# Down projection of a decoder layer: a third piece in four by seven products, some subtractions on GpSimd

## The chip, the cores and the metric

One core of one Trainium2 chip runs one decoder layer on 256 positions. The metric is the device time of one execution in microseconds, median of three runs. TensorE does the matmuls, VectorE (DVE) and ScalarE (ACT) the elementwise work, GpSimd (POOL) a little, and SyncE (SP) issues nearly all DMAs.

## What is computed

```
x <- LayerNorm(ALPHA * x + token_mixer(x))          # three branches, then w_out
x <- LayerNorm(ALPHA * x + swiglu_ffn(x))

def swiglu_ffn(x, w_gu, w_down):
    gate, up = split(x @ w_gu, 2)                   # 2048 -> 2 x 5632
    return (silu(gate) * up) @ w_down               # 5632 -> 2048
```

All is float32, and only the last line, the down projection of the feed-forward part, changes in how it is computed.

## The kernel before

**Matmuls in split form.** Each float32 operand is split into a high part (rounded to the fp32r format, by a ScalarE copy) and a low part (operand minus high part, a VectorE subtraction). A product is three matmuls: high by high, high by low, low by high.

**Pieces.** All weights stream through as pieces of 256 rows by 512 columns, laid out as 128 x 1024 (512 KB). A `Job` is a run of pieces with one accumulator. One list, `pieces`, fixes the order of the whole program; nothing is reordered later. For piece i the main loop does, in this order: issue loads (`advance`), split the piece three ahead (`advance_split`; its high part is copied one piece earlier still), the matmuls of piece i (`mults`), one waiting small task (`later`), and, at the last piece of a job, its evacuation (`job.evac`). VectorE and ScalarE work through their instructions in this order. There are 6 buffers for raw pieces, 5 for high parts (`wh`) and 4 for low parts (`wl`), so the low part of a piece can be written when the piece four before it has been multiplied.

**The feed-forward stage.** The hidden width is cut into 11 blocks of 512. Block b has a gate job and an up job of 8 pieces each (form A). From block 2 on, `weave` (L1062) puts four pieces of the down projection (form B) into each such job, one after every second piece: blocks 2 and 3 carry the down pieces of the hidden pair 0 and 1, blocks 4 and 5 those of the pair 2 and 3, and so on, one quarter of the 2048 output columns per job. That makes 18 woven jobs. The rest of the down projection follows by itself at the end (`down`, L1051).

**Seven products.** An ordinary form-B piece multiplies a 256 x 256 block of the hidden values by a 256 x 512 block of weights with 12 matmuls of 512 columns (`mul_b`, L1159). Two of the four down pieces of a woven job, k = 1 and 2, instead use Strassen's seven products of 128 x 128 by 128 x 256 (`mul_seven`, L1185), 21 matmuls of 256 columns. This needs sums of the four weight blocks, which `split_lo` (L1129) makes on VectorE (L1145 to L1147), splits (L1148, and `split_from` twice, L203 and L204) and puts into a slot that alternates between `h0` and `s5`; and sums of the hidden blocks, which `ev_ffup` makes for odd blocks only (`sums`, L895 to L903). Even blocks only split their hidden values.

**Accumulators.** PSUM has three double banks `acc` and two single banks `tr`. A woven job's form-A part uses two of the `acc`. Its down part uses the third (`ab`) and, for the seven products, both `tr` banks (`c` and `d`, taken by the first product piece). `ev_seven` (L928) evacuates them: L935 (L933 for the first pair) adds `ab`; L937 copies `d` on ScalarE; L939 to L941 form differences; L942 adds the first half of `c`, which is the last read of that bank; L943 and L944 add the rest. The first matmul of `mul_seven` writes `c`.

**At the end of a job** the order of VectorE's work is: evacuation of the form-A part (L616, for an up job with L889), split of the next job's first down piece, for an up job the split or the sums of the first half of its hidden values, and then `ev_seven`.

Of the kernel before, what the change touches and what calls it, by code (L numbers as in the profile page):

```python
# [12 lines left out]
F32R = mybir.dt.float32r  # L13
I32 = mybir.dt.int32
AF = mybir.ActivationFunctionType
ALU = mybir.AluOpType
# [3 lines left out]
P = 128  # L20
NT = 2
T = 256
KT = D // P
DFF = 5632
NB = DFF // 512
# [23 lines left out]
class Job:  # L49
    def __init__(self, form, src, act, n, evac, needs=None, bias=None, done=None, post=None, late=None, own=None, banks=False, split=False, seven=()):  # L50
        self.form = form
        self.src = src
        self.act = act
        self.n = n
        self.evac = evac
        self.needs = needs or {}
        self.post = post or {}
        self.bias = bias
        self.done = done
        self.ps = [None, None]  # L60
        self.cd = None
        self.bc = None
        self.late = late or ()
        self.own = own or {}
        self.banks = banks
        self.split = split
        self.seven = seven


class Act:  # L70
# [35 lines left out]
def layer_kernel(ctx: ExitStack, tc: tile.TileContext, xT_d, mem_d, memT_d, wi_d, wif_d, wkv_d,  # L106
                 wpa_d, wpb_d, wpc_d, wout_d, wgu_d, wdn_d, pp_d, bif_d, gws_d, gbs_d, bin_d, gln_d, xr_d, lnp_d, out_d):
    nc = tc.nc
    ve, ac, te, gp, sy = nc.vector, nc.scalar, nc.tensor, nc.gpsimd, nc.sync
# [12 lines left out]
    def nm(s):  # L122
        cnt[0] += 1
        return f"{s}{cnt[0]}"

    def slot(tag, shape, dt=F32):
        return big.tile(shape, dt, tag=tag, name=nm(tag))

    def t2(shape=None, dt=F32):
        return tmp.tile(shape or [P, 512], dt, tag="t2", name=nm("t2"))  # L130
# [4 lines left out]
    def bc2():  # L135
        return tmp.tile([P, 512], F32, tag="bc", name=nm("bc"), bufs=2)
# [7 lines left out]
    def two(a):  # L144
        return a.rearrange("p (a b) -> p a b", a=2)

    def flat(a):
        return a.rearrange("p a b -> p (a b)")
# [53 lines left out]
    def split_from(src, hi_ap, lo_ap):  # L202
        ac.activation(hi_ap, src, AF.Copy)  # L203
        ve.tensor_sub(lo_ap, src, hi_ap)  # L204
# [49 lines left out]
    S = {}  # L254
# [370 lines left out]
    def once(key, make):  # L625
        if key not in S:
            S[key] = make()
        return S[key]
# [243 lines left out]

    later = []

    def ev_ffup(b):
        def f(job, hf):
            g = S["hid", b][:, 2 * hf:2 * hf + 2]
            odd = b % 2
            if hf == 0:
                if odd:  # L880
                    h = slot(("s3", "s1")[b // 2 % 2], [P, 2, 2, 8, P], F32R)
                else:
                    h = slot(("s6", "s6b")[b // 2 % 2], [P, 2, 2, 2, T], F32R)
                for i in range(2):
                    S["hT", b, i] = h[:, i]
            h = S["hT", b, hf]
            u = two(t2())
            comb(job, hf, u)
            ve.tensor_mul(g, g, u)  # L889
            if h.shape[2] != 8:  # L890
                later.append(lambda: split_from(g, h[:, :, 0], h[:, :, 1]))
                return
            a = flat(g).rearrange("p (a b) -> p a b", a=4)

            def sums():  # L895
                ac.activation(h[:, 0, 0:4], a, AF.Copy)
                s = t2([P, 4, P])
                ve.tensor_tensor(s[:, 0:2], a[:, 1:2].to_broadcast([P, 2, P]), a[:, 0:4:3], ALU.subtract)
                ve.tensor_sub(s[:, 2], a[:, 0], s[:, 1])
                ve.tensor_sub(s[:, 3], a[:, 2], s[:, 2])  # L900
                ac.activation(h[:, 0, 4:8], s, AF.Copy)
                ve.tensor_sub(h[:, 1, 0:4], a, h[:, 0, 0:4])
                later.insert(0, lambda: ve.tensor_sub(h[:, 1, 4:8], s, h[:, 0, 4:8]))  # L903

            later.append(sums)
        return halves(f)

    def ev_down(b, j, first, last):
# [19 lines left out]
    def ev_seven(j, first):  # L928
        def f(job):
            a = S["acc"][:, :, j * 512:(j + 1) * 512]  # L930
            ab, (c, d) = job.ps[0], job.cd
            if first:
                ve.scalar_tensor_tensor(a, a, ALPHA, ab, ALU.mult, ALU.add)  # L933
            else:
                ve.tensor_add(a, a, ab)  # L935
            e = t2()
            ac.activation(e, d, AF.Copy)  # L937
            w, z = t2(), t2([P, 2, T])
            ve.tensor_sub(w[:, 0:T], c[:, 0:T], e[:, 0:T])  # L939
            ve.tensor_sub(w[:, T:], w[:, 0:T], e[:, T:])  # L940
            ve.tensor_tensor(z, c[:, T:].unsqueeze(1).to_broadcast([P, 2, T]), two(w), ALU.subtract)  # L941
            ve.tensor_add(a[:, 0, T:], a[:, 0, T:], c[:, 0:T])  # L942
            ve.tensor_add(a[:, 1, T:], a[:, 1, T:], w[:, T:])  # L943
            ve.tensor_add(a[:, :, 0:T], a[:, :, 0:T], z)  # L944
        return f
# [115 lines left out]

    def weave(up, b0, j):  # L1062

        act = lambda: Hid([S["hT", b0, 0], S["hT", b0 + 1, 0], S["hT", b0 + 1, 1], S["hT", b0, 1]])
        src = [wdn_d[j, 2 * b0 + i] for i in (0, 2, 3, 1)]
        dn = Job("B", src, act, 4, ev_seven(j, b0 == 0), seven=(1, 2))
        for k in range(8):
            pieces.append((up, k))
            if k % 2 == 1:
                pieces.append((dn, k // 2))  # L1070

    for b in range(NB):
        n = {k: (lambda kk: (lambda: x1_unit(kk + 2)))(k) for k in range(6)} if b == 0 else None
        gate = Job("A", wgu_d[b], lazy("x1T"), 8, ev_ffgate(b), post=n, done=start("x1", task_x1) if b == 0 else None)
        up = Job("A", wgu_d[NB + b], lazy("x1T"), 8, ev_ffup(b), needs={7: lambda: drain("x1")} if b == 1 else None)
# [9 lines left out]
    raw, hl, owned, cur, n7 = {}, {}, {}, [0], [0]  # L1085
# [47 lines left out]
    def split_lo(i):  # L1133
        l = owned.pop(i) if i in owned else wp.tile([P, 1024], F32R, tag="wl", name=nm("wl"))
        r = raw.pop(i)
        hl[i][1] = l
        job, k = pieces[i]
        if k not in job.seven:
            ve.tensor_sub(l, r, hl[i][0])  # L1139
            return  # L1140
        n7[0] += 1
        s = slot(("h0", "s5")[n7[0] % 2], [P, 2, 1024], F32R)
        hl[i].append(s)
        p, q = bc2(), bc2()
        ve.tensor_tensor(two(p), r[:, 0:T].unsqueeze(1).to_broadcast([P, 2, T]), two(r[:, T:3 * T]), ALU.add)  # L1145
        ve.tensor_add(q[:, 0:T], p[:, 0:T], r[:, 2 * T:3 * T])
        ve.tensor_add(q[:, T:], q[:, 0:T], r[:, 3 * T:])  # L1147
        ve.tensor_sub(l[:, T:], r[:, T:], hl[i][0][:, T:])  # L1148
        split_from(p, s[:, 0, 0:512], s[:, 1, 0:512])
        split_from(q, s[:, 0, 512:], s[:, 1, 512:])  # L1150
# [6 lines left out]
    def mul_b(job, k, h, l, t, half=None):  # L1157
        a = job.act()
        o, n = 0, 512  # L1159
        if job.split and t == 1:  # L1160
            if half is None:
                mul_b(job, k, h, l, t, 0)
                mul_b(job, k, h, l, t, 1)
                return
            if job.ps[1] is None:
                job.ps[1] = [bank(), bank()]
            ps = job.ps[1][half][:, 0:T]
            o, n = half * T, T
        elif job.banks:
            if job.ps[t] is None:  # L1170
                job.ps[t] = bank()
            ps = job.ps[t]
        else:
            ps = acc(job, 0)[:, t]
        for j in range(2):
            kt = 2 * k + j
            wh, wl = h[:, j * 512 + o:j * 512 + o + n], l[:, j * 512 + o:j * 512 + o + n]
            f, e = k == 0 and j == 0, k == job.n - 1 and j == 1
            te.matmul(ps, a.sta(kt, 0, t), wh, start=f, stop=False)  # L1179
            te.matmul(ps, a.sta(kt, 0, t), wl, start=False, stop=False)  # L1180
            te.matmul(ps, a.sta(kt, 1, t), wh, start=False, stop=e)  # L1181

    def mul_seven(job, k, h, l, s):

        a = job.act().pairs[k]  # L1185
        ab = acc(job, 0)
        first = job.cd is None
        if first:
            job.cd = [bank(), bank()]
        c, d = job.cd  # L1190
        end = k == job.seven[-1]
        w = lambda i: (h[:, i * T:(i + 1) * T], l[:, i * T:(i + 1) * T])
        u = lambda i: (s[:, 0, i * T:(i + 1) * T], s[:, 1, i * T:(i + 1) * T])

        def prod(out, i, b, start=False, stop=False):
            te.matmul(out, a[:, 0, i], b[0], start=start, stop=False)  # L1196
            te.matmul(out, a[:, 0, i], b[1], start=False, stop=False)  # L1197
            te.matmul(out, a[:, 1, i], b[0], start=False, stop=stop)  # L1198

        prod(c[:, 0:T], 0, w(1), start=first)  # L1200
        prod(ab[:, 0, T:], 2, w(3))
        prod(ab[:, 0, 0:T], 7, w(2))
        prod(c[:, T:], 5, u(0), stop=end)
        prod(d[:, T:], 4, u(1), start=first)
        prod(d[:, 0:T], 6, u(2), stop=end)
        prod(ab[:, 1, T:], 3, u(3))

    def mul_a(job, k, h, l, hf, w, j):
        a, kt = job.act(), 2 * k + j
# [80 lines left out]
    for i in range(N):  # L1290
        job, k = pieces[i]
# [79 lines left out]
```

## Time and profile before

| | us |
|---|---|
| median of 3 runs (1840.77 to 1841.02) | 1841.02 |
| the profiled execution | 1840.85 |
| its span, first to last instruction | 1839.1 |
| TensorE busy | 1823.3 (99%) |
| VectorE busy | 1283.1 (70%) |
| ScalarE busy | 945.9 (51%) |
| GpSimd busy | 9.5 (1%) |

The mean granted clock of TensorE is 0.998. A busy share is an average over the run; matmuls are pipelined, so that the durations of neighbouring ones overlap and the interval from start to start is what one costs. VectorE's operations overlap a little too.

### The profile page before, as it was taken

Reading aid. Unit: us, or ns where it says so; the run is one execution under the profiler, and the core shown is the slowest. Engines: PE = TensorE matmul, PEld = TensorE weight load, DVE = VectorE, ACT = ScalarE, POOL = GpSimd, SP = SyncE. Lnnn points to the kernel's source line nnn. Section 1 sums busy time; section 2 is a strip of 40 time slices with the busy share of each in tenths; the row PEclk is TensorE's granted clock in tenths of the full one; section 3 lists DMA queues with packets and bytes.
Section 4 is the critical chain, followed back from the end, with each engine's and each line's share of the span. In section 5 each row is a group of like instructions: output and inputs, shape, how many; then the busy total and the mean of one; then the engine's idle time right before and its main releaser. Section 6 shows DMA issues by size and latency. Waiting matters only on the chain.

```text
span 1839.1 us, 26103 instructions
## 1 busy us (share of the span) xinstructions
PE 1823.3 (99%) x10154; PEld 1575.3 (86%) x10154; DVE 1283.1 (70%) x1741; ACT 945.9 (51%) x1147; POOL 9.5 (1%) x24
## 2 busy tenths in 40 slices
PE   9999999999999999999999999999999999999997
PEld 8888888888888888888888888888888888888886
DVE  6886566557667666565555568577877878878787
ACT  6554465555555555544444355455555555555453
POOL 0000000000000000000000000000000000000001
PEclk9999999999999999999999999999999999999999
DMA  9666555555555555655556645665565565566656
GB/s 373 216 223 189 182 171 165 181 166 189 163 188 162 176 191 164 185 186 169 190 189 239 243 158 172 189 200 184 171 219 171 185 217 181 184 196 197 194 173 182
DMA packets 97627, 352.64 MB, mean 192 GB/s; under 512 B 10848, under 2 KB 11360, under 8 KB 96352
## 3 DMA queue, kind: packets, MB, share of 16 engines
q1 hardware_dynamic: 96496, 348.89, 58.5%
q0 software_dynamic: 576, 1.05, 0.5%
q8 instruction: 79, 1.29, 0.3%
q10 hardware_dynamic: 432, 1.05, 0.2%
q14 instruction: 44, 0.36, 0.1%
HBM read 348.85 MB, written 3.15 MB: 191 GB/s over the span
## 4 chain that ended last, share of the span: by engine, by line
PE 97%; DVE 2%; ACT 0%; DMA 0%; issue 0%; SPq 0%; DVEq 0%; ACTq 0%
PE acc L1214 45%; PE acc L1216 23%; PE acc L1181 7%; PE acc L1180 7%; PE acc L1179 7%; PE tr L1198 1%; PE tr L1196 1%; PE tr L1197 1%; PE acc L1198 1%; PE acc L1197 1%; PE acc L1196 1%; DVE wl L1139 1%; PE tr L198 1%; PE tr L199 0%; PE tr L200 0%; DVE t L841 0%
## 5 line engine op out<-in xcount | busy, mean ns | idle before, releaser
L1214 PE MATMUL acc<-s,wh 128*128 128x512 f32 x3520 | 966.2, 396 | 2.5 <-DVE s L846 1.1
L1139 DVE TENSOR_TENSOR wl<-raw,wh 128x1024 fp32r<-128x1024 f32 x589 | 712.3, 1222 | 362.8 <-PE acc L1216 180.9
L1120 ACT ACTIVATE wh<-raw 128x1024 fp32r<-128x1024 f32 x589 | 618.9, 1058 | 566.0 <-PE acc L1214 344.9
L1214 PEld LDWEIGHTS acc<-s,wh 128*128 128x128 f32 x3520 | 602.5, 188 | 86.6 <-DVE s L846 1.4
L1216 PEld LDWEIGHTS acc<-s,wl 128*128 128x128 f32 x3520 | 542.2, 189 | 80.9 <-DVE wl L1139 0.5
L1216 PE MATMUL acc<-s,wl 128*128 128x256 f32 x3520 | 560.8, 281 | 0.1
L1181 PE MATMUL acc<-wh,s 128*128 128x512 f32 x452 | 179.4, 397 | 0.0
L1179 PE MATMUL acc<-wh,s 128*128 128x512 f32 x452 | 179.0, 396 | 0.0
L1180 PE MATMUL acc<-wl,s 128*128 128x512 f32 x452 | 178.2, 394 | 0.0
L1181 PEld LDWEIGHTS acc<-wh,s 128*128 128x128 f32 x452 | 84.9, 188 | 20.4
L1180 PEld LDWEIGHTS acc<-wl,s 128*128 128x128 f32 x452 | 84.9, 188 | 19.4
L1179 PEld LDWEIGHTS acc<-wh,s 128*128 128x128 f32 x452 | 85.0, 188 | 18.6
L616 DVE TENSOR_TENSOR g<-g,acc 128x512 f32<-128x512 f32 x54 | 37.2, 688 | 50.3 <-ACT g L615 34.6
L615 ACT ACTIVATE g<-acc,pp 128x256 f32<-128x256 f32 x64 | 26.9, 472 | 28.9 <-PE acc L1216 28.9
L1118 ACT ACTIVATE wh<-raw 128x768 fp32r<-128x768 f32 x36 | 30.4, 845 | 18.4 <-PE acc L1214 11.7
L1181 PE MATMUL acc<-wh,s6b 128*128 128x512 f32 x96 | 38.1, 397 | 0.0
L1180 PE MATMUL acc<-wl,s6b 128*128 128x512 f32 x96 | 38.0, 396 | 0.0
L1179 PE MATMUL acc<-wh,s6b 128*128 128x512 f32 x96 | 37.8, 394 | 0.0
L612 ACT ACTIVATE t<-acc 128x512 f32<-128x512 f32 x38 | 22.7, 598 | 27.3 <-PE acc L1216 27.3
L616 DVE TENSOR_TENSOR t<-t,acc 128x512 f32<-128x512 f32 x38 | 26.1, 686 | 13.7 <-ACT t L612 13.7
L1148 DVE TENSOR_TENSOR wl<-raw,wh 128x768 fp32r<-128x768 f32 x36 | 34.3, 953 | 0.8
L203 ACT ACTIVATE s<-bc 128x512 fp32r<-128x512 f32 x36 | 22.8, 633 | 19.3 <-DVE bc L1145 15.2
(336 smaller groups left out, 1505.0 us busy)
## 6 DMA issues: line engine op xcount, KB each, us to landing
raw<-in_wi SPq DMA_DIRECT2D x238, 512.0 KB, 3.7
raw<-in_wgu SPq DMA_DIRECT2D x176, 512.0 KB, 4.2
raw<-in_wdn SPq DMA_DIRECT2D x88, 512.0 KB, 3.8
raw<-in_wkv SPq DMA_DIRECT2D x32, 512.0 KB, 3.6
raw<-in_wpb SPq DMA_DIRECT2D x32, 512.0 KB, 4.4
raw<-in_wout SPq DMA_DIRECT2D x32, 512.0 KB, 3.6
raw<-in_wpa SPq DMA_DIRECT2D x16, 512.0 KB, 3.6
raw<-in_wpc SPq DMA_DIRECT2D x16, 512.0 KB, 3.6
```

The source lines that it names most:

```text
L616: ve.tensor_add(out, out, ps[:, :, 0:T])
L1120: ac.activation(h, r, AF.Copy)
L1139: ve.tensor_sub(l, r, hl[i][0])
L1148: ve.tensor_sub(l[:, T:], r[:, T:], hl[i][0][:, T:])
L1179: te.matmul(ps, a.sta(kt, 0, t), wh, start=f, stop=False)
L1180: te.matmul(ps, a.sta(kt, 0, t), wl, start=False, stop=False)
L1181: te.matmul(ps, a.sta(kt, 1, t), wh, start=False, stop=e)
L1196: te.matmul(out, a[:, 0, i], b[0], start=start, stop=False)
L1197: te.matmul(out, a[:, 0, i], b[1], start=False, stop=False)
L1198: te.matmul(out, a[:, 1, i], b[0], start=False, stop=stop)
L1214: te.matmul(ps, w[:, o:o + P], a.both(kt), start=k == 0 and j == 0, stop=False)
L1216: te.matmul(ps[:, 0:T], w[:, o:o + P], a.hi(kt), start=False, stop=k == job.n - 1 and j == 1)
```

## The change

In woven jobs of the blocks from 4 on (the hidden pairs from block 2 on), the order of the four down pieces becomes (1, 2, 3, 0) and the first three of them go by seven products; the fourth is ordinary. The first product piece starts the accumulator, with start flags on the parts that it writes first, and the ordinary piece splits one of its matmuls into two halves of 256 columns, since one half of that bank has not been written by then. The pair of blocks 0 and 1 keeps its order and its two product pieces. To feed a third product piece, the second half of the hidden values of the blocks 2, 4, 6 and 8 is also kept with its sums; their first half moves into a part of a new tile, `lot`, that takes the whole slot `s5` and also holds every second set of weight sums. In all 18 woven jobs the low parts of the form-A pieces 2 and 3 are subtracted by GpSimd in place of VectorE, and that of the last down piece too where three pieces go by seven products.

```diff
--- before.py
+++ after.py
@@ -65,6 +65,7 @@
         self.banks = banks
         self.split = split
         self.seven = seven
+        self.aside = ()
 
 
 class Act:
@@ -872,17 +873,26 @@
 
     later = []
 
+    def lot():
+        return once("lot", lambda: slot("s5", [P, 4096], F32R))
+
     def ev_ffup(b):
         def f(job, hf):
             g = S["hid", b][:, 2 * hf:2 * hf + 2]
-            odd = b % 2
+            q = b // 2 % 2
             if hf == 0:
-                if odd:
-                    h = slot(("s3", "s1")[b // 2 % 2], [P, 2, 2, 8, P], F32R)
+                if b % 2:
+                    h = slot(("s3", "s1")[q], [P, 2, 2, 8, P], F32R)
+                    hs = h[:, 0], h[:, 1]
+                elif b in (0, NB - 1):
+                    h = slot(("s6", "s6b")[q], [P, 2, 2, 2, T], F32R)
+                    hs = h[:, 0], h[:, 1]
                 else:
-                    h = slot(("s6", "s6b")[b // 2 % 2], [P, 2, 2, 2, T], F32R)
+                    h = slot(("s6", "s6b")[q], [P, 2, 8, P], F32R)
+                    o = (2 + q) * 1024
+                    hs = lot()[:, o:o + 1024].rearrange("p (k a t) -> p k a t", k=2, a=2), h
                 for i in range(2):
-                    S["hT", b, i] = h[:, i]
+                    S["hT", b, i] = hs[i]
             h = S["hT", b, hf]
             u = two(t2())
             comb(job, hf, u)
@@ -1061,9 +1071,12 @@
 
     def weave(up, b0, j):
 
-        act = lambda: Hid([S["hT", b0, 0], S["hT", b0 + 1, 0], S["hT", b0 + 1, 1], S["hT", b0, 1]])
-        src = [wdn_d[j, 2 * b0 + i] for i in (0, 2, 3, 1)]
-        dn = Job("B", src, act, 4, ev_seven(j, b0 == 0), seven=(1, 2))
+        o, seven = ((0, 2, 3, 1), (1, 2)) if b0 == 0 else ((1, 2, 3, 0), (0, 1, 2))
+        act = lambda: Hid([S["hT", b0 + i // 2, i % 2] for i in o])
+        src = [wdn_d[j, 2 * b0 + i] for i in o]
+        dn = Job("B", src, act, 4, ev_seven(j, b0 == 0), seven=seven)
+        up.aside = (2, 3)
+        dn.aside = (3,) if len(seven) == 3 else ()
         for k in range(8):
             pieces.append((up, k))
             if k % 2 == 1:
@@ -1136,10 +1149,13 @@
         hl[i][1] = l
         job, k = pieces[i]
         if k not in job.seven:
-            ve.tensor_sub(l, r, hl[i][0])
+            (gp if k in job.aside else ve).tensor_tensor(l, r, hl[i][0], ALU.subtract)
             return
         n7[0] += 1
-        s = slot(("h0", "s5")[n7[0] % 2], [P, 2, 1024], F32R)
+        if n7[0] % 2:
+            s = lot()[:, 0:2048].rearrange("p (a b) -> p a b", a=2)
+        else:
+            s = slot("h0", [P, 2, 1024], F32R)
         hl[i].append(s)
         p, q = bc2(), bc2()
         ve.tensor_tensor(two(p), r[:, 0:T].unsqueeze(1).to_broadcast([P, 2, T]), two(r[:, T:3 * T]), ALU.add)
@@ -1176,7 +1192,11 @@
             kt = 2 * k + j
             wh, wl = h[:, j * 512 + o:j * 512 + o + n], l[:, j * 512 + o:j * 512 + o + n]
             f, e = k == 0 and j == 0, k == job.n - 1 and j == 1
-            te.matmul(ps, a.sta(kt, 0, t), wh, start=f, stop=False)
+            if 0 in job.seven and t == 1 and j == 0:
+                for x in (0, T):
+                    te.matmul(ps[:, x:x + T], a.sta(kt, 0, t), wh[:, x:x + T], start=False, stop=False)
+            else:
+                te.matmul(ps, a.sta(kt, 0, t), wh, start=f, stop=False)
             te.matmul(ps, a.sta(kt, 0, t), wl, start=False, stop=False)
             te.matmul(ps, a.sta(kt, 1, t), wh, start=False, stop=e)
 
@@ -1184,7 +1204,7 @@
 
         a = job.act().pairs[k]
         ab = acc(job, 0)
-        first = job.cd is None
+        first, lead = job.cd is None, k == 0
         if first:
             job.cd = [bank(), bank()]
         c, d = job.cd
@@ -1198,12 +1218,12 @@
             te.matmul(out, a[:, 1, i], b[0], start=False, stop=stop)
 
         prod(c[:, 0:T], 0, w(1), start=first)
-        prod(ab[:, 0, T:], 2, w(3))
+        prod(ab[:, 0, T:], 2, w(3), start=lead)
         prod(ab[:, 0, 0:T], 7, w(2))
         prod(c[:, T:], 5, u(0), stop=end)
         prod(d[:, T:], 4, u(1), start=first)
         prod(d[:, 0:T], 6, u(2), stop=end)
-        prod(ab[:, 1, T:], 3, u(3))
+        prod(ab[:, 1, T:], 3, u(3), start=lead)
 
     def mul_a(job, k, h, l, hf, w, j):
         a, kt = job.act(), 2 * k + j
```

## Rows read from the trace of the kernel before

**Rows 1.** The page, part 1: busy us, share of the span, instructions.

```profile
PE 1823.3 (99%) x10154; PEld 1575.3 (86%) x10154; DVE 1283.1 (70%) x1741; ACT 945.9 (51%) x1147; POOL 9.5 (1%) x24
```

**Rows 2.** Waits of TensorE: line, waited for; us in total, times, longest us.

```profile
PE acc L1214 <- DVE s L846: 1.1, 1, 1.1
```

**Rows 3.** Windows: us; PE, PEld, DVE, ACT, POOL busy (count); clock; DMA share, GB/s.

```profile
1452.00:1485.00 33.00, 33.00 (x195) 29.02 (x195) 28.55 (x42) 17.32 (x23) 0.00 (x0) 1.00 0.60 191
1485.00:1518.00 33.00, 33.00 (x195) 29.07 (x194) 24.78 (x34) 17.67 (x23) 0.00 (x0) 1.00 0.59 192
```

**Rows 4.** Timeline (start us, us, engine, line, operation, count): a product, an ordinary piece.

```profile
1407.97 0.28 PE L1196 MATMUL tr<-wh,s 128*128 128x256 f32 x1
...
1410.48 1.09 PE L1214 MATMUL acc<-s,wh 128*128 128x512 f32 x4
...
1416.12 0.39 PE L1179 MATMUL acc<-wh,s6b 128*128 128x512 f32 x1
...
1418.93 1.08 PE L1214 MATMUL acc<-s,wh 128*128 128x512 f32 x4
```

**Rows 5.** Timeline of VectorE: the split of one product piece and what follows.

```profile
1491.59 0.69 DVE L1145 TENSOR_TENSOR bc<-raw 128x512 f32<-128x512 f32 x1
...
1493.98 1.29 DVE L204 TENSOR_TENSOR s<-bc,s 128x512 fp32r<-128x512 f32 x2
1495.19 1.22 DVE L1139 TENSOR_TENSOR wl<-raw,wh 128x1024 fp32r<-128x1024 f32 x1
```

**Rows 6.** Timeline of TensorE: one dn3, dn0 behind odd up, gate, even up.

```profile
1449.26 0.39 PE L1179 MATMUL acc<-wh,s6b 128*128 128x512 f32 x1
...
1457.67 0.39 PE L1179 MATMUL acc<-wh,s 128*128 128x512 f32 x1
...
1490.81 0.39 PE L1179 MATMUL acc<-wh,s 128*128 128x512 f32 x1
...
1523.94 0.39 PE L1179 MATMUL acc<-wh,s 128*128 128x512 f32 x1
```

**Rows 7.** Timeline of VectorE at the same three boundaries.

```profile
1451.42 1.22 DVE L1139 TENSOR_TENSOR wl<-raw,wh 128x1024 fp32r<-128x1024 f32 x1
1452.55 0.42 DVE L898 TENSOR_TENSOR t<-g 128x256 f32<-128x256 f32 x1
...
1456.79 0.41 DVE L942 TENSOR_TENSOR s<-s,tr 128x256 f32<-128x256 f32 x1
...
1483.82 1.22 DVE L1139 TENSOR_TENSOR wl<-raw,wh 128x1024 fp32r<-128x1024 f32 x1
1485.39 1.22 DVE L935 TENSOR_TENSOR s<-s,acc 128x1024 f32<-128x1024 f32 x1 [0.35 <-PE acc L1181]
...
1488.05 0.41 DVE L942 TENSOR_TENSOR s<-s,tr 128x256 f32<-128x256 f32 x1
...
1522.07 0.41 DVE L942 TENSOR_TENSOR s<-s,tr 128x256 f32<-128x256 f32 x1
```

**Rows 8.** Timeline of ScalarE behind the gate job.

```profile
1484.91 1.04 ACT L1120 ACTIVATE wh<-raw 128x1024 fp32r<-128x1024 f32 x1
```

**Rows 9.** Timeline, all engines: VectorE's end and TensorE's next weight load.

```profile
1092.52 0.88 DVE L846 TENSOR_TENSOR s<-t,s 128x256 fp32r<-128x256 f32 x2
...
1093.45 0.31 PEld L1214 LDWEIGHTS acc<-s,wh 128*128 128x128 f32 x2 [0.15 <-DVE s L846]
```

**Rows 10.** Timeline of GpSimd: its two widest operations.

```profile
123.97 2.10 POOL L300 TENSOR_SCALAR_AFFINE_SELECT wT<-wT 128x1024 f32<-128x1024 f32 x1 [121.04 <-DMA wT<-in_gws]
...
1833.09 1.27 POOL L978 TENSOR_TENSOR s<-s,s 128x512 f32<-128x512 f32 x1 [3.65 <-ACT s L974]
```

**Rows 11.** Timeline of VectorE beside the first of them.

```profile
123.90 1.21 DVE L1139 TENSOR_TENSOR wl<-raw,wh 128x1024 fp32r<-128x1024 f32 x1
```

**Rows 12.** Timeline of TensorE: the second piece of the first gate job.

```profile
1096.27 1.18 PE L1214 MATMUL acc<-s,wh 128*128 128x512 f32 x4
```

**Rows 13.** Timeline of VectorE: a later part of the same stationary tile.

```profile
1098.44 0.69 DVE L204 TENSOR_TENSOR s<-t,s 128x512 fp32r<-128x512 f32 x1 [0.70 <-ACT s L203]
```

## The prediction

> **What bounds the kernel now.** I read the busy shares first. TensorE is busy for 1823.3 of 1839.1 us [rows 1], but matmuls overlap, so that alone proves little. The list of what TensorE waited for settles it: its largest wait for another engine after the start is 1.1 us in the whole run, once [rows 2]. So the sum of TensorE's issue intervals is the time, and another engine matters only where it makes TensorE wait. In the stage of the change (gate and up jobs with down-projection pieces between) a 33 us window shows TensorE full at a granted clock of 1.00, its 2.4 GHz level, VectorE busy for 24.8 to 28.6 us, ScalarE for 17.3 to 17.7, GpSimd for nothing [rows 3]. Averages leave room everywhere. The question is whether they leave it at the place where the work is added, so I then followed VectorE in order of time around the end of a job.
>
> I call the four down pieces of a job dn0 to dn3 and its eight others g0 to g7. The order is g0 g1 dn0 g2 g3 dn1 g4 g5 dn2 g6 g7 dn3.
>
> **What the third product piece gives.** An ordinary piece holds TensorE from 1416.12 to 1418.93, 2.81 us for 12 matmuls of 512 columns; a seven-product piece from 1407.97 to 1410.48, 2.51 us for 21 of 256 [rows 4]. The blocks from 2 on have 14 such jobs (gate and up of 4 to 9 are twelve, those of 10 two more); blocks 0 and 1 keep two product pieces. In each of the 14 one piece changes: 14 x 0.30 = 4.2 us less. The ordinary piece that remains splits one 512-column matmul in two: 2 x 2.51/21 - 2.81/12 = 0.005 us, 0.07 in all. Net gain 4.1 us, and no more, since TensorE waits for nothing in this stage that the change could take away.
>
> **What it costs VectorE and ScalarE.** A seven-product split holds VectorE from 1491.59 to 1495.19, 3.60 us start to start [rows 5]; a plain one from 1451.42 to 1452.55, 1.13 us [rows 7]. So VectorE pays 14 x 2.47 = 35 us, and is spared 50 plain subtractions (three in each of 18 jobs, less four in blocks 0 and 1), 56 us. The second half of four even blocks now also makes sums: L942 ends 3.07 us behind the start of the evacuation (1488.46 less 1485.39), so behind the odd block the evacuation began at 1457.20 - 3.07 = 1454.13 and the sums before it, from 1452.55, took 1.58 us [rows 7]; four times that is 6 us. In total VectorE does less, and that total decides nothing, as it is not the bound. ScalarE gains about 1 us a job, two half-width copies for a narrower wide one, and has 15 us of room [rows 3].
>
> **GpSimd's subtractions.** No row has the operation in this width. The nearest is its 128x512 tensor_tensor, 1.27 us; doubled 2.54 is the upper end, and its one-input pass over 128x1024, 2.10 us, the lower [rows 10]. I take 2.4. The low-part buffer that g2 of the next job needs comes free as dn3 ends, and TensorE wants it after g0, g1 and dn0: 8.41 - 2.81 + 2.51 = 8.1 us later [rows 4, 6]. The same holds for g3, and for dn3 between dn2 and g6, g7. So its latency is hidden up to three times my value, and I price it at nothing on TensorE's side.
>
> **The step on the path.** dn0 becomes a product piece. Its first matmul writes one of the two banks that the previous job's products were summed in, and there are only two. They come free when VectorE has done the fifth operation of the evacuation, L942. Before, dn0 needed only the other accumulator, and the banks were wanted at dn1, over 8 us later. And VectorE works in order: after the evacuation of g7 it splits the next dn0, then makes the sums of an up job, then evacuates dn3. That split is now 2.47 us longer and stands right in front. The three kinds of boundary:
>
> - Behind an up job of an odd block L942 ends at 1456.79 + 0.41 = 1457.20 [rows 7] and dn0 starts at 1457.67 [rows 6]: slack 0.47. VectorE has no gap in this chain, so it moves by 2.47. With 0.05 us from VectorE's end to TensorE's next start (1093.40 to 1093.45 [rows 9]) the stall is 2.47 + 0.05 - 0.47 = 2.05 us. Four such boundaries (blocks 3, 5, 7, 9): 8.2 us.
> - Behind an up job of an even block only half of one split stands there: L942 ends at 1522.48, dn0 starts at 1523.94, slack 1.46, stall 1.06. Three (4, 6, 8): 3.2 us. The new sums of the even blocks come after the evacuation and don't lengthen it.
> - Behind a gate job VectorE is free at 1483.82 + 1.13 = 1484.95 and waits until 1485.39 for dn3. The new split would end at 1483.82 + 3.60 = 1487.42, but its two copies on ScalarE stand behind the one from 1484.91 to 1485.95 [rows 8], which with the first copy (about 0.6, an estimate from the 0.6 of VectorE's subtraction of the same width in [rows 5]) adds some 0.3: the evacuation starts at 1487.74 and L942 ends at 1490.81. dn0 starts at 1490.81: stall 0.05, between none and 0.4. Seven (4 to 10): 0.4 us.
>
> Sum 11.7 us. Behind the stall dn1 is the next to be late: VectorE goes on from 1457.20 + 2.47 = 1459.67 with the rest of the evacuation (0.4 + 0.6), a difference (0.6; widths as in [rows 5, 7]) and the second sums (1.58), to 1462.9, then with its split, to 1466.5; TensorE wants it at 1457.67 + 2.05 + 2.51 + 5.60 = 1467.8, so 1.3 us are left. That is what taking g2 and g3 off VectorE buys: with their 2 x 1.13 us, 1.0 would be missing there. It comes after the evacuation in VectorE's order and does nothing for the wait at dn0.
>
> The forecast for the profiled execution is 1840.85 - 4.1 + 11.7 = 1848.4; it stands 0.17 below the median of the runs, so 1848.6. The likeliest case's own range is 1845 to 1853: ScalarE's order can move each boundary by some 0.3 us, and 14 x 0.3 = 4.
>
> **Rivals.** *A port held by GpSimd.* A subtraction of GpSimd that runs beside the chain may hold up VectorE's operations with two SBUF inputs, which are all those of the split. The one for g2 can start as dn3 ends, in the middle of the split of dn0. If VectorE loses one such operation of 2.4 us at each of 14 boundaries, the stalls are 4.45, 3.46 and 2.45: 45 us, and the time 1882; if the one for g3, 5.6 us later, does it too, 14 x 2.4 more, 1916. For it: nothing in this kernel shows two such operations together. Against it: beside GpSimd's pass from 123.97 to 126.07 [rows 10] VectorE's two-input subtraction took its usual 1.21 us [rows 11], but it had started 0.07 us earlier. It decides as soon as GpSimd wins the start. The Trainium skill (SBUF — State Buffer, "Who interferes with whom") says just that: a VectorE instruction with two SBUF inputs contends with a GpSimd one that reads SBUF, and whichever starts first blocks the other for its whole length. The row is at one with that for VectorE coming first, and can't show the other order; by the page the time would be that of this rival. I give the rival less than one in four, since it is open which of the two starts first at 14 places.
>
> *Faster.* The added split hides after all. VectorE is idle for whole microseconds inside each job; were the split of dn0 ready before the evacuation of g7, the chain behind dn3 would be as it was, dn0 would find its banks free with 0.47 to 2.35 us to spare, and the 4.1 us would stay: 1836.9. It decides where the chain moves by less than 0.5 us. Against it: in the trace the split of dn0 stands behind the evacuation in all three kinds [rows 7].
>
> *Within the noise.* The stall exists but is about a third of what I work out (1 us behind odd blocks, nothing elsewhere): 1840.9. It wants 1 us of VectorE's chain to overlap that I count as serial.
>
> *One tile for two things.* Half of an even block's hidden values and every second product split now share one tile. If readers of one part waited for writers of the other, dn3 would wait for the split of a later piece, about 3 us in 14 jobs: 1890. Against it: TensorE began a piece at 1096.27 that reads the tile of which another part was written at 1098.44, by an earlier instruction of the program [rows 12, 13].
>
> **Chances.** Forecast 0.45, port 0.23, faster 0.13, within the noise 0.14, one tile 0.05. What a measurement of this kernel tells from no change is about 0.2%, 3.7 us. So faster 0.13, same 0.14, slower 0.73. The range 1836.5 to 1883 holds the forecast, both cases below it and the milder half of the port's, about 0.83.
>
> **What would show it.** Right: idle time of TensorE before the first 256-column matmul of dn0, released by the evacuation's addition of the first bank, about 2.05, 1.06 and 0.05 us by kind of block; 50 product splits in place of 36; TensorE's time for the pieces down by 4.1 us. Port: subtractions on VectorE of over 1.5 us, or GpSimd's of over 3 us, where they overlap. Tile: waits of TensorE in dn3 for the product split. Wrong: no idle time at dn0, or stalls that sit at dn1 or at g2 and g3 (GpSimd over 8 us late).

## The result, and the profile after

The changed kernel takes 1886.81 us (median of 4 runs, 1885.77 to 1890.14) where the kernel before takes 1841.02 beside it: 1.0252 times as long, 95% interval 1.0234 to 1.0270. The forecast was 1848.6 with a range up to 1883. The span grew from 1839.1 to 1886.0 us, by 46.9.

TensorE now waits in the stage of the change. The waits of TensorE, as in [rows 2] (us in total, times, longest; L945, L947 and L952 are what L935, L937 and L942 were):

```profile
PE acc L1216 <- DVE s L945: 14.6, 10, 1.8
PE tr L1216 <- DVE s L952: 8.3, 13, 1.3
PE tr L1216 <- ACT t L947: 6.1, 4, 1.5
```

All of it is dn0 waiting for the evacuation of the job before. (These 29.0 us are idle time between the recorded, modelled ends and starts of matmuls; the loss counted from start to start further down is larger.) The timeline of VectorE behind a gate job, to be held against the gate rows of [rows 7], shows why it comes so late:

```profile
1428.25 0.69 DVE L1161 TENSOR_TENSOR bc<-raw 128x512 f32<-128x512 f32 x1
1428.97 0.42 DVE L1162 TENSOR_TENSOR bc<-bc,raw 128x256 f32<-128x256 f32 x1
...
1429.78 0.95 DVE L1164 TENSOR_TENSOR wl<-raw,wh 128x768 fp32r<-128x768 f32 x1
1430.93 5.43 DVE L205 TENSOR_TENSOR h<-bc,h 128x512 fp32r<-128x512 f32 x2 [0.20 <-ACT h L204]
1436.28 1.21 DVE L945 TENSOR_TENSOR s<-s,acc 128x1024 f32<-128x1024 f32 x1
...
1438.93 0.41 DVE L952 TENSOR_TENSOR s<-s,tr 128x256 f32<-128x256 f32 x1
```

and the timeline of GpSimd over the same microseconds:

```profile
1430.51 5.29 POOL L1152 TENSOR_TENSOR wl<-raw,wh 128x1024 fp32r<-128x1024 f32 x2 [9.12 <-ACT wh L1133]
```

The last two subtractions of the split took 5.43 us; in [rows 5] the same pair took 1.29. They lie over GpSimd's subtractions for g2 and g3 (1430.51 to 1435.80), and the evacuation starts at 1436.28, when GpSimd is done. Behind an up job one operation of the split is held in the same way; VectorE and GpSimd behind block 3:

```profile
1320.57 2.52 DVE L1163 TENSOR_TENSOR bc<-bc,raw 128x256 f32<-128x256 f32 x1
```

```profile
1320.19 2.62 POOL L1152 TENSOR_TENSOR wl<-raw,wh 128x1024 fp32r<-128x1024 f32 x1 [27.45 <-DVE bc L1161]
```

TensorE at the first of these two boundaries, the gate one, in order of time:

```profile
1435.26 0.28 PE L1216 MATMUL tr<-wh,s6b 128*128 128x256 f32 x1
...
1437.55 0.39 PE L1216 MATMUL acc<-wh,s6b 128*128 128x256 f32 x1 [1.77 <-DVE s L945]
...
1439.39 0.39 PE L1216 MATMUL tr<-h,s6b 128*128 128x256 f32 x1 [0.52 <-DVE s L952]
...
1440.57 1.09 PE L1234 MATMUL acc<-s,wh 128*128 128x512 f32 x4
```

dn0 takes 5.31 us from its first matmul to the first of g2, where a product piece takes 2.51: 2.80 us of stall. The new first bank was free at once here, and the waits are for the second of the seven products (`ab`, L945) and the fifth (the other bank, L952).

At another gate boundary something comes on top. The stretches of 2 us of TensorE (us, busy and count, granted clock, DMA share, GB/s), and two of its matmuls:

```profile
1506.00:1508.00 2.00, 2.00 (x16) 1.00 0.81 215
1508.00:1510.00 2.00, 0.24 (x3) 1.00 0.62 129
1510.00:1512.00 2.00, 1.48 (x10) 0.94 0.57 227
1512.00:1514.00 2.00, 2.00 (x10) 0.50 0.00 0
1514.00:1516.00 2.00, 2.00 (x10) 0.71 0.00 0
1516.00:1518.00 2.00, 2.00 (x12) 1.00 0.86 248
```

```profile
1512.45 0.42 PE L1218 MATMUL tr<-h,s 128*128 128x256 f32 x1
1512.66 0.41 PE L1216 MATMUL tr<-h,s 128*128 128x256 f32 x1
```

After the idle time the granted clock falls to half, the 1.2 GHz level, and 256-column matmuls follow each other every 0.21 us instead of every 0.12, until the clock is back some 3 us later. Taking each boundary's excess over 2.51 us for dn0 and 5.64 us for the two pieces on either side, the 14 boundaries cost 49.4 us. The five of them with no slow matmuls show 2.80 us (gate, one), 2.54 (even, one) and 2.77 (odd, three). If the stalls of the other nine are as long as these, 7, 3 and 4 boundaries would cost 38.3, and the slow matmuls of the nine account for about 11 us (an estimate); the mean granted clock of the run is 0.989, before 0.998. The 49.4 less the gain of the third product (3 to 4 us) is, within a microsecond, the 46.9.

### The profile page after: what moved, and what is told of

Its sections match the earlier page's. It is cut to its first block, busy times and chain, and to the rows that moved or that the text cites. A ratio compares the mean times of both kernels' runs of the same rounds, so it can differ in the third digit from the quotient of the medians.

```text
span 1886.0 us, 26580 instructions
## 1 busy us (share of the span) xinstructions
PE 1840.9 (98%) x10294; PEld 1593.7 (85%) x10294; DVE 1348.7 (72%) x1777; ACT 956.0 (51%) x1179; POOL 136.3 (7%) x74
## 4 chain that ended last, share of the span: by engine, by line
PE 89%; DVE 10%; ACT 1%; DMA 0%; issue 0%; SPq 0%; DVEq 0%; ACTq 0%
PE acc L1234 41%; PE acc L1236 21%; PE acc L1201 6%; PE acc L1200 6%; PE acc L1199 6%; DVE h L205 2%; PE tr L1216 1%; PE tr L1218 1%; PE tr L1217 1%; DVE bc L1163 1%; PE acc L1216 1%; PE acc L1218 1%; PE acc L1217 1%; DVE s L205 1%; DVE s L945 1%; DVE wl L1152 1%
## 5 line engine op out<-in xcount | busy, mean ns | idle before, releaser
L1152 DVE TENSOR_TENSOR wl<-raw,wh 128x1024 fp32r<-128x1024 f32 x525 | 657.4, 1263 | 343.9 <-PE acc L1236 182.5
L1133 ACT ACTIVATE wh<-raw 128x1024 fp32r<-128x1024 f32 x575 | 602.3, 1055 | 498.7 <-PE acc L1234 270.9
L1152 POOL TENSOR_TENSOR wl<-raw,wh 128x1024 fp32r<-128x1024 f32 x50 | 127.2, 2552 | 1109.1 <-PE acc L1236 852.0
L204 ACT ACTIVATE s<-bc 128x512 fp32r<-128x512 f32 x50 | 31.6, 632 | 76.9 <-DVE bc L1161 55.6
L1131 ACT ACTIVATE wh<-raw 128x768 fp32r<-128x768 f32 x50 | 41.9, 839 | 47.7 <-PE acc L1234 38.7
L205 DVE TENSOR_TENSOR h<-bc,h 128x512 fp32r<-128x512 f32 x50 | 61.2, 1264 | 2.4 <-ACT h L204 1.4
L1164 DVE TENSOR_TENSOR wl<-raw,wh 128x768 fp32r<-128x768 f32 x50 | 47.6, 951 | 0.0
L1163 DVE TENSOR_TENSOR bc<-bc,raw 128x256 f32<-128x256 f32 x50 | 35.9, 717 | 1.7
```

Of the source, the lines that this page charges most:

```text
L1131: ac.activation(h[:, T:], r[:, T:], AF.Copy)
L1133: ac.activation(h, r, AF.Copy)
L1152: (gp if k in job.aside else ve).tensor_tensor(l, r, hl[i][0], ALU.subtract)
```

## The experiments

Two theories stood at the start. A: GpSimd's subtractions hold up VectorE's operations with two SBUF inputs, and TensorE's clock falls behind the stalls. B: the longer split in front of the evacuation is the whole cause and GpSimd is harmless. The excess of pieces is counted as above throughout.

**Without GpSimd** (from the changed kernel):

```diff
-        up.aside = (2, 3)
-        dn.aside = (3,) if len(seven) == 3 else ()
```

> The changed kernel with all 50 subtractions back on VectorE; three product pieces stay. Theory A (GpSimd's subtractions hold up VectorE's operations with two SBUF inputs in the chain in front of dn0, and TensorE's clock falls after the stalls): no VectorE operation is longer than in the kernel before; what is left of the stall is 0.6 us at dn0 behind odd blocks and about 1 us at dn1 behind up jobs, some 8 us, less the 4.1 us gained: 1845, clock back near 0.998. Theory B (the longer split in front of the evacuation is the whole cause, GpSimd is harmless): stalls of about 2 us at each of the 14 boundaries stay and VectorE has 56 us more to do: 1885 or more.

Measured: 1846.31 us, 1.0028 times before (1.0017 to 1.0039); 40 us came back with the 50 subtractions, though VectorE has them to do again. No operation of VectorE in this stage takes over 1.23 us, as in the kernel before; in the changed kernel 46 take over 1.5. The waits of TensorE in this stage:

```profile
PE tr L1215 <- DVE wl L1162: 3.8, 7, 0.7
PE tr L1214 <- DVE s L952: 1.8, 4, 0.5
```

The first is dn1 waiting for its own split behind the seven up jobs, the second dn0 behind the four odd ones. In piece times: 0.70 us at dn0 and 0.96 up to and in dn1 behind odd blocks, 0.66 at dn1 behind even ones, nothing behind gate jobs, 8.6 us in all. Granted clock 0.998. Theory B is out.

**GpSimd alone** (from the kernel before: two product pieces, dn0 ordinary):

```diff
+        self.aside = ()
...
+        up.aside = (2, 3)
+        dn.aside = (3,) if b0 else ()
...
-            ve.tensor_sub(l, r, hl[i][0])
+            (gp if k in job.aside else ve).tensor_tensor(l, r, hl[i][0], ALU.subtract)
```

> The kernel before with only the 50 subtractions moved to GpSimd; two product pieces everywhere. Theory A: single VectorE operations of 2.5 to 2.9 us appear at the ends of the jobs, beside GpSimd's; as dn0 is ordinary there and has slack, most of it is hidden: 1841 to 1850. Theory B: no VectorE operation is lengthened, 1841.

Measured: 1841.52 us, 1.0003 (0.9993 to 1.0012). The same holds are there and cost nothing. VectorE and GpSimd behind a gate job:

```profile
1419.58 1.22 DVE L936 TENSOR_TENSOR s<-s,acc 128x1024 f32<-128x1024 f32 x1 [0.35 <-PE acc L1184]
1420.72 0.42 DVE L940 TENSOR_TENSOR t<-tr,t 128x256 f32<-128x256 f32 x1
1421.17 1.80 DVE L941 TENSOR_TENSOR t<-t,t 128x256 f32<-128x256 f32 x1
1423.02 0.69 DVE L942 TENSOR_TENSOR t<-tr,t 128x512 f32<-128x512 f32 x1
```

```profile
1420.28 4.96 POOL L1142 TENSOR_TENSOR wl<-raw,wh 128x1024 fp32r<-128x1024 f32 x2 [9.12 <-ACT wh L1123]
```

This tells which operations are held. L936, L940 and L942 read one input from PSUM (`acc`, `tr`) and take their 1.22, 0.42 and 0.69 us in the midst of GpSimd's work. L941 reads two tiles in SBUF and takes 1.80 where 0.43 is usual. And what frees `ab`, the only bank that an ordinary dn0 wants, is of the first kind: dn0 is 0.05 us late behind odd blocks and on time elsewhere.

**GpSimd in the middle of a job:**

```diff
-        up.aside = (2, 3)
+        up.aside = (6, 7)
```

> The changed kernel with GpSimd's subtractions for the form-A pieces 6 and 7 in place of 2 and 3, so that they run in the middle of a job and not beside the chain in front of dn0. Theory A: holds of VectorE move to the middle of the job, where it has room; at the boundary what is left is as in the kernel without GpSimd: 1846 to 1852. Theory B: nothing changes at the boundary, 1887.

Measured: 1848.44 us, 1.0039 (1.0023 to 1.0054). The holds moved, as in VectorE's split of a dn2:

```profile
1405.61 2.88 DVE L1161 TENSOR_TENSOR bc<-raw 128x512 f32<-128x512 f32 x1
1408.53 0.43 DVE L1162 TENSOR_TENSOR bc<-bc,raw 128x256 f32<-128x256 f32 x1
```

There VectorE has room; only behind odd blocks are 0.5 us lost later in the job. The excess is 10.7 us, against 8.6 without GpSimd.

**One of the two.** Only g3, or only g2, on GpSimd, beside dn3 (below, the edit for g3; for g2 it is `(2,)`):

```diff
-        up.aside = (2, 3)
+        up.aside = (3,)
```

> The changed kernel with the subtraction for g2 back on VectorE; those for g3 and dn3 stay on GpSimd. Theory A: GpSimd can start on g3 only when g0 has been multiplied, 5.6 us behind the start of dn3. Behind a gate job the split of dn0 is over by then and the evacuation reads PSUM, so nothing in front of dn0 is held; behind an up job one hold of about 2.2 us remains. Stalls 0 to 0.5 (gate), 2 to 2.8 (odd), 1 to 1.8 (even): 1850 to 1857. Theory D (each GpSimd subtraction costs the same wherever it runs): two thirds of the loss, 1872.

> The changed kernel with the subtraction for g3 back on VectorE; those for g2 and dn3 stay on GpSimd. Theory A: GpSimd starts on g2 as dn3 ends, in the middle of the split of dn0, and holds VectorE once for some 2.2 us at all 14 boundaries: stalls of 0.8 (gate), 1.7 (even) and 2.7 us (odd), 22 us, and a little at dn1: 1860 to 1866 with some of the clock's loss. Theory D: 1872.

Measured: g3 only 1848.05 us, 1.0038 (1.0023 to 1.0053); g2 only 1859.31 us, 1.0099 (1.0084 to 1.0114). Both lie below the ranges expected, 1850 to 1857 and 1860 to 1866. Per boundary dn0 with g2 alone lasts 0.58 us too long (gate), 1.78 (even) and 2.78 (odd, with the wait in front of it, three of four; at the fourth, where the clock fell, 3.87), each within about 0.2 us of what was expected. With g3 alone the gate boundaries lose 0.17 us, as expected, but the others less than that: 0.53 (even) and 1.90 (odd, 0.70 of it at dn0 and the rest while TensorE waits for g2's own split, which VectorE reaches behind the held operation). The expectation had a full hold of 2.2 us in front of dn0 behind up jobs; there GpSimd started once the evacuation had begun, and of the hold only 0.8 us (even) or nothing (odd) lies in front of the release of the bank that dn0 waits for. With g3 alone, behind a gate job, VectorE and GpSimd:

```profile
1422.15 1.29 DVE L205 TENSOR_TENSOR h<-bc,h 128x512 fp32r<-128x512 f32 x2 [0.21 <-ACT h L204]
1423.36 1.21 DVE L945 TENSOR_TENSOR s<-s,acc 128x1024 f32<-128x1024 f32 x1
...
1424.94 1.89 DVE L950 TENSOR_TENSOR t<-t,t 128x256 f32<-128x256 f32 x1
```

```profile
1424.14 2.40 POOL L1152 TENSOR_TENSOR wl<-raw,wh 128x1024 fp32r<-128x1024 f32 x1 [10.90 <-ACT wh L1133]
```

The split is through before GpSimd starts, and one hold of 1.46 us lands in the evacuation. Theory D, that a subtraction costs the same wherever it runs, would have both at 1872 and is out. Against the kernel without GpSimd g3 costs 1.7 us (within what the intervals leave open), g2 13 us and both 40.5; dn3 is on GpSimd in all three, and from dn2 to the end of a job no piece is late in any of them. The two add up to more than their sum: with g2's hold in front, g3's falls into the same chain and adds 2.2 us at a gate boundary (0.58 to 2.80) and 0.76 at an even one (1.78 to 2.54), nothing at an odd one, and the clock comes on top.

**Filling the stall.** In the changed kernel TensorE repeats a matmul while it waits.

```diff
+        self.fill = (0, 0)
...
+        if b0:
+            dn.fill = (16, 5) if j % 2 else ((7, 12) if j else (0, 9))
...
         prod(c[:, 0:T], 0, w(1), start=first)
+        for _ in range(job.fill[0] if lead else 0):
+            te.matmul(c[:, 0:T], a[:, 0, 0], w(1)[0], start=False, stop=False)
...
         prod(c[:, T:], 5, u(0), stop=end)
+        for _ in range(job.fill[1] if lead else 0):
+            te.matmul(c[:, T:], a[:, 0, 5], u(0)[0], start=False, stop=False)
```

> The changed kernel with matmuls repeated while TensorE waits in dn0 (their results are added to the first product bank, so the output is not the reference's): 16 and 5 behind gate jobs, 7 and 12 behind up jobs of even blocks, none and 9 behind those of odd blocks, of 0.12 us each, about as long as the two waits there. Theory A (the stall is VectorE's chain, held by GpSimd; on top of it TensorE's clock falls behind part of the stalls, some 11 us): the stalls stay as filled time, granted clock back at 0.998, 1875 to 1879. Theory C (the slow matmuls behind the stalls are not the clock's, or the clock falls for another reason than idle time): clock stays at 0.989 and the time at 1887 or, with the repeated matmuls in the way, above.

Measured: 1878.88 us, 1.0204 (1.0187 to 1.0221), 7.9 us below the changed kernel, though TensorE has more to do. The granted clock (the figure behind the five busy times) over the stage, first of this kernel and then of the changed one:

```profile
1320.00:1440.00 120.00, 118.46 (x744) 106.21 (x743) 105.32 (x134) 60.90 (x80) 28.85 (x11) 1.00 0.53 175
1440.00:1560.00 120.00, 118.50 (x735) 106.46 (x735) 101.66 (x133) 61.01 (x80) 22.73 (x9) 0.99 0.52 170
```

```profile
1320.00:1440.00 120.00, 111.36 (x662) 98.27 (x661) 103.21 (x130) 60.00 (x78) 27.98 (x11) 0.97 0.53 171
1440.00:1560.00 120.00, 113.82 (x683) 100.96 (x682) 101.15 (x132) 59.67 (x79) 22.71 (x9) 0.97 0.54 168
```

So most of the 11 us was the clock, and it fell because TensorE stood idle; what is left is the stall itself. The clock is 0.996 over the whole run, not 0.998: behind odd blocks the wait comes before dn0's first matmul and could not be filled this way, and one of these four boundaries still shows slow matmuls.

**The third product in another place.** From the changed kernel, without GpSimd, dn0 stays ordinary:

```diff
-        o, seven = ((0, 2, 3, 1), (1, 2)) if b0 == 0 else ((1, 2, 3, 0), (0, 1, 2))
+        o, seven = ((0, 2, 3, 1), (1, 2)) if b0 == 0 else ((0, 1, 2, 3), (1, 2, 3))
...
+        last = k == job.n - 1
-        prod(ab[:, 0, 0:T], 7, w(2))
+        prod(ab[:, 0, 0:T], 7, w(2), stop=last)
...
-        prod(ab[:, 1, T:], 3, u(3), start=lead)
+        prod(ab[:, 1, T:], 3, u(3), start=lead, stop=last)
```

> Three product pieces as in the changed kernel, but they are the last three of four (dn0 ordinary, order 0, 1, 2, 3) and no subtraction is on GpSimd. dn0 then needs no product bank and its split in front of the evacuation is the short one. Both theories: TensorE loses the 4.1 us of the third product and nothing waits: 1837. If VectorE is too full for a third product wherever it stands: waits at dn3, 1841 or more.

Measured: 1837.33 us (11 runs, 1836.49 to 1837.87), 0.9978 (0.9969 to 0.9987), the only version that beats the kernel before, by 0.2%. TensorE waits for nothing in the stage, with VectorE at 27.7 to 31.1 of 33 us:

```profile
1452.00:1485.00 33.00, 33.00 (x206) 29.52 (x205) 31.08 (x48) 18.61 (x25) 0.00 (x0) 1.00 0.58 191
1485.00:1518.00 33.00, 33.00 (x205) 29.57 (x204) 27.67 (x38) 18.43 (x25) 0.00 (x0) 1.00 0.62 192
```

## Why the prediction was wrong

Its direction held, its size did not: 7.6 us were forecast and 46 came.

*The gain of the third product* was about right: 4.1 us forecast, 4.0 measured between the medians where nothing waits (3.2 between the spans of the two profiles). The piece times say a little less than the forecast: a job, from dn0 to dn0, takes 33.13 us before, 32.86 in the last kernel above and 32.89 in the changed order where nothing waits. That is 0.24 to 0.27 us a job and not 0.30, or 3.4 to 3.8 in 14, as the two pieces behind a product piece take 5.64 us and behind an ordinary one 5.62.

*GpSimd's subtractions* is the step that failed. Their duration was right (2.4 forecast, 2.38 to 2.42 where nothing held them), in part by luck, since the 2.10 that served as its lower end was itself a held time, as shown below. Their own slack was right too: TensorE never waits for one of them. But "I price it at nothing on TensorE's side" counted only who waits for the result, not whom the operation holds while it runs. That stood among the rivals at 0.23, priced at 1882 for one hold and 1916 for two, and it is what came: behind gate jobs both holds fall into the chain, behind up jobs one in front of the evacuation. With it the stalls are 38 us instead of 8.6. That 1886.81 lies so near the rival's 1882 is partly luck: its stalls were 45 us in place of 38, and it had no term for the 11 us of the clock.

The row that I weighed on the other side was itself a held operation. GpSimd's pass of 2.10 us [rows 10] ran beside VectorE's subtraction [rows 11], and I took VectorE's usual 1.21 us for a sign of peace. In the last kernel above the same pass happened to run after the subtraction, beside statistics with one input:

```profile
126.13 1.09 POOL L301 TENSOR_SCALAR_AFFINE_SELECT wT<-wT 128x1024 f32<-128x1024 f32 x1 [123.22 <-DMA wT<-in_gws]
```

```profile
124.64 1.21 DVE L1150 TENSOR_TENSOR wl<-raw,wh 128x1024 fp32r<-128x1024 f32 x1
125.77 1.28 DVE L310 BATCH_NORM_STATS2 st<-s 128x6 f32<-128x512 f32 x2
```

It took 1.09 us. So in the kernel before GpSimd had waited 1.0 us for VectorE, inside its recorded 2.10: VectorE had come first, and the two could not run together. In the changed kernel the same pass starts later beside the same subtraction and takes 1.74, and in both it ends 0.95 or 0.96 us behind the end of VectorE's operation:

```profile
124.43 1.21 DVE L1152 TENSOR_TENSOR wl<-raw,wh 128x1024 fp32r<-128x1024 f32 x1
```

```profile
124.86 1.74 POOL L301 TENSOR_SCALAR_AFFINE_SELECT wT<-wT 128x1024 f32<-128x1024 f32 x1 [121.94 <-DMA wT<-in_gws]
```

The Trainium skill (SBUF — State Buffer, "Who interferes with whom") has the rule that decides: a VectorE instruction with two SBUF inputs contends with a GpSimd one that reads SBUF, the ports that they share are an exclusive lock, and the order of issue decides who blocks. (That the other one blocks in full it says of VectorE's two-port modes.) The runs agree for two SBUF inputs in both directions, VectorE's 2.52 for 0.43 us and GpSimd's 2.10 for 1.09, and also in the exception, at most one input from SBUF: 1.22, 0.42 and 0.69 us beside GpSimd's work.

*The step on the path* was right in kind, but too large and not at its places. That its 11.7 us stand near the 8.6 without GpSimd is luck: only 2.8 of the 8.6 (4 x 0.70) are at dn0. It said that dn0's first matmul writes the bank which L942 frees. The trace shows it waiting for ScalarE's copy instead (L947, four times 1.5 us): the new first bank is the old second one. The bank that the addition frees is wanted only by the fifth of seven products, 12 matmuls or 1.43 us later. So dn0 behind odd blocks lost 0.70 us and not 2.05, and the gate and even cases nothing. The rest, 0.66 to 0.96 at dn1, is no part of that step; it is what the prediction named as missing there with g2 and g3 on VectorE (1.0).

*The clock* was not in the sum. It had been 1.00 in the stage before [rows 3], and the sum has no term for a fall behind stalls of 2 us. It cost about 11 us, 8 of them shown by the filled stalls.

*The shared tile* cost nothing: no wait of TensorE in dn3 in any run.

## What to carry to other kernels

Work moved to GpSimd had two prices here: the wait for its result, and the time for which it holds VectorE's operations with two SBUF inputs; so it belongs where VectorE is not in a chain that TensorE waits for, or beside operations that read PSUM. Before an accumulator is wanted earlier in a job, add up in order everything that its evacuation stands behind, and look which buffer the new one really takes. Stalls of 2 to 3 us in a loop that keeps TensorE full can cost more than their length, because the clock falls behind some of them: here about 11 us on top of 38.

## What the runs showed of the hardware

- A VectorE operation of 128x512 with two SBUF inputs, 0.69 us by itself, took 2.88 beside a GpSimd subtraction that had started before it; a 128x256 one 2.52 in place of 0.43. Two GpSimd subtractions back to back let one VectorE operation through between them: 5.43 us for a pair of 1.29.
- The hold is mutual. GpSimd's 128x1024 subtraction takes 2.38 to 2.42 us where nothing holds it and up to 3.48 where VectorE came first; its 128x1024 select 1.09, or 1.74 and 2.10 where VectorE came first.
- After 1.9 and 0.7 us without matmuls, with 1.1 us of them between, TensorE's granted clock stood at 0.50 for about 3 us; at other boundaries of nearly the same shape it stayed at 1.00. Which of the two happens is not settled by these runs.
